# One decoder layer on one Trainium2 core: the order of work around three RMS norms, the opening products behind them, and the split of four weight blocks

## The chip, the cores and the metric

The kernel runs on one core of a Trainium2 chip (trn2). The metric is device time in microseconds (us) of one execution. A core has a matrix engine (PE in the profile), a vector engine (DVE), an activation engine (ACT), a general engine (POOL) and a sync engine (SP), each of which runs its own row of instructions in order, and 16 DMA engines. The profile shows a granted clock of the matrix engine (PEclk); 1.00 is its full 2.4 GHz, and the other level is 1.2 GHz.

## The reference

One layer on 512 prompt tokens and 8 x 4 sample tokens, 544 in all, with 1024 features: a half-step SwiGLU block, a mixer (RWKV-7 heads beside differential attention), a second SwiGLU block, and an RMS norm ahead of and behind each of the three.

```python
def rms_norm(x, g, eps):
    return x * lax.rsqrt(jnp.mean(x * x, axis=-1, keepdims=True) + eps) * g

def swiglu(x, w_in, w_out):
    gate, up = jnp.split(x @ w_in, 2, axis=-1)
    return (jax.nn.silu(gate) * up) @ w_out

def layer(x, l, shift0, wkv0, attend, P):
    g = P['norm_gains'][l]
    h = x + 0.5 * rms_norm(swiglu(rms_norm(x, g[0]), ff1_in, ff1_out), g[1])
    m, k, v, wkv, shift = mixer(rms_norm(h, g[2]), l, shift0, wkv0, attend, P)
    h = h + rms_norm(m, g[3])
    h = h + 0.5 * rms_norm(swiglu(rms_norm(h, g[4]), ff2_in, ff2_out), g[5])
    return h, k, v, wkv, shift
```

Here `D_FF` is 2816 and everything is fp32.

## The kernel before, in words

Features lie on partitions, tokens on the free axis. The 544 tokens are two halves of 272 (`HALF`), s = 0 and s = 1, and an activation is KB = 8 tiles of 128 x 272 for each half. Every fp32 product is made of three products of a rounded high part and a low part: high weight by high input, high weight by low input, low weight by high input.

**Weights.** `weights()` (L110 to L126) loads 128 x 1024 fp32 (512 KB) by SP into `wraw` (3 buffers), ACT copies it into the high part `whi` (L118), and DVE subtracts to get the low part `wlo` (L124). `whi` and `wlo` have 4 buffers each, so at most four blocks are ready at a time. With `added=True` the low part is made without DVE: ACT writes the negated copy (L121), and POOL issues a DMA that adds the weights from memory onto it (L122).

**Products.** `dot` (L134) is one 128-feature output for one half: 16 matmuls with `whi` (L138 with the high input `xh`, L139 with the low input `xl`), then 8 with `wlo` (L142), all into one PSUM bank. `acc_tile` hands out three PSUM banks in turn (names mm and pb). `mm3` (L128) is the same for a single tile.

**Norms.** For y, the output of a block, `Squares` accumulates squares (ACT squares, DVE or POOL adds, L236); the accumulators are `sqa0` and `sqa1`. `rstds` (L238) takes the sums over partitions with ones on PE (L176, 3 columns of tokens), computes 1/sqrt with ten small DVE instructions (`inv_sqrt`, L200 to L210, on 128 x 3) and spreads the result over partitions by PE transposes (`spread`, L222). `close_half` (L270) then does, tile by tile, norm (`pn`, L284), residual add into `h` (L285; POOL for tiles 0, 2, 4, 6, DVE for the others), the parts `xh` (ACT, L254) and `xl` (DVE, L256) of the next block's input, and the squares of the new h. These steps are a generator that later products advance (`tick`). The scale of the next norm is not put into the parts but applied to the products behind them. `Pre.scale` (L259) makes it: for the norms ahead of both SwiGLU blocks (`gi` 0 and 4) by one matmul with a 128 x 128 matrix of ones (L263) and `inv_sqrt` on the wide 128 x 272 form; for the mixer's norm (`gi` 2) by `rstds` and an ACT copy.

**What follows a norm.** `opening` (L316) is the first four products of the next block: for half 0 four whole dots, with half 1's norm steps advanced between them, then half 1 tile by tile in four banks (`mm3`). `after(...)` pins matmuls behind others on PE: `chain` holds the last transpose and the last sum matmul of half 1's norm. In `ff` the opening makes gate and up of output blocks j = 0 and 1; they are copied to SBUF, and scaled once the scale is there (L520, L521). Blocks j = 2 to 5 of the first group go one at a time: two weight blocks (gate, up), half 0, then half 1, and here DVE takes the products out of PSUM by a multiplication with the scale (L530, L531), which therefore has to be there. DVE then multiplies gate and up (L407), and the low part of the hidden tile is made (L151). `scaled` and `mixtures` (L372, L363, L365, L385) prepare tiles for the later groups.

**Order.** The Tile framework simulates the program and writes each engine's row from it, by priority and readiness, so the order on an engine is not the order of the text. The norm before ff2 lies behind `w_out` (L1378 to L1392: eight dots for half 0, eight for half 1; in half 1 the weights m > 3 have `added=True`).

Of the kernel before, what the change touches and what calls it, by code (L numbers as in the profile page):

```python
# [13 lines left out]
OP = mybir.AluOpType  # L14
# [38 lines left out]
def build(ctx, tc, A):  # L53
# [191 lines left out]
    class Pre:  # L245
# [12 lines left out]

        def scale(self, s):  # L259
            self.rs[s] = wk.tile([128, HALF], FT, name=f"rpre{s}", bufs=1)  # L260
            if self.gi != 2:
                ps = bank()
                T.matmul(ps[:, :HALF], ones, self.sq[s].acc, start=True, stop=True)  # L263
                inv_sqrt(ps, HALF, 1.0 / DM, NORM_EPS, y=self.rs[s])
            else:
                S.activation(self.rs[s], rstds(self.sq[s])[0], AF.Copy)
# [3 lines left out]
    def close_half(h, s, y, sq, gcol, pre=None, xp=None, spill=None, out=None, pool=True):  # L270

        drain()
        if s == 1 and pre is not None:
            with tc.high_priority():
                r, = rstds(sq)
            chain[:] = last
            pre.scale(0)
        else:
            r, = rstds(sq)

        def steps():
            for m in range(KB):
                t = wk.tile([128, HALF], FT, name="pn")
                V.scalar_tensor_tensor(t, y[s][m], gcol[:, m:m + 1], r, op0=OP.mult, op1=OP.mult)  # L284
                (G if m in ((0, 2, 4, 6) if out is None else (0, 2, 4)) else V).tensor_tensor(h[s][:, m], h[s][:, m], t, op=OP.add)  # L285
                if out is not None and (m % 2 or m == KB - 2):
                    q = m if m >= KB - 2 else m - 1
                    nc.sync.dma_start(out[s, :, q:m + 1], h[s][:, q:m + 1])
                if pre is not None:
                    pre.split(xp, h, s, m)  # L290
                    pre.sq[s].add(h[s][:, m], G if pool and s == 0 and m in (2, 4, 6) else V)
                if spill is not None and m % 2:
                    nc.scalar.dma_start(spill[s, :, m - 1:m + 1], h[s][:, m - 1:m + 1])
                yield
            if s == 1 and pre is not None:
                pre.scale(1)

        later.append(steps())

# [16 lines left out]
    def opening(ws, xs, take):  # L316

        for i, w in enumerate(ws):
            ps = acc_tile()
            with after(chain[1] if i == 1 else chain[0] if i == 2 else None):  # L320
                dot(ps, w, xs[0])
            take(0, i, ps)
            tick(3)
# [69 lines left out]
    def ff(win, wout, pre, h, done, xp, end, lead=(), begin=None):  # L393
        with ExitStack() as st:
# [112 lines left out]
            for gi, (j0, j1) in enumerate(GROUPS):  # L507
                if gi == 0:
# [9 lines left out]
                    for s in range(2):  # L518
                        for g, u in raw[s]:
                            V.tensor_tensor(g, g, pre.rs[s], op=OP.mult)  # L520
                            V.tensor_tensor(u, u, pre.rs[s], op=OP.mult)  # L521
                            hidden(s, g, u)
                    for j in range(2, j1):
                        ws = [weights(win[j, i], 1024) for i in range(2)]
                        for s in range(2):
                            pg, pu = acc_tile(), acc_tile()
                            for p, w in zip((pg, pu), ws):
                                dot(p, w, pre.xs[s])
                            g, u = gate_up()
                            V.tensor_tensor(g, pg, pre.rs[s], op=OP.mult)  # L530
                            V.tensor_tensor(u, pu, pre.rs[s], op=OP.mult)  # L531
                            hidden(s, g, u)
                            for _ in range(3 * (j > 2)):
                                next(scaled, None)
                else:
                    for j in range(j0, j1):
                        now = ahead or seven(j)
# [840 lines left out]
    def output(s):  # L1378
# [1 line left out]
            t = (s4 if j == 2 else c4)([128, 3, HALF], f"my{s}_{j}")  # L1380
            y[s].extend(t[:, m] for m in range(3))
        for m in range(KB):
            w = weights(A["w_out"][m], 1024, added=s == 1 and m > 3)
            ps = acc_tile()
            dot(ps, w, parts[s])
            S.activation(y[s][m], ps, AF.Copy)
# [172 lines left out]
```

## Time and profile before

| | us |
|---|---|
| median of three timed runs | 1233.25 (1227.38 to 1235.25) |
| the profiled execution | 1238.08 |
| its span in the trace | 1236.3 |
| PE busy | 1182.9 (96%) |
| DVE busy | 827.9 (67%) |
| ACT busy | 580.2 (47%) |
| POOL busy | 183.6 (15%) |

In the rows below times are us from the start of the span unless marked ns. A timeline row gives start, duration, engine, line, operation, output<-inputs, shapes and count; in brackets the idle time of the engine ahead of it and what ended it. A window row gives for a stretch the busy time of PE, the PE weight loads, DVE, ACT and POOL (with the number of instructions), then the granted clock, the DMA share and GB/s. Durations of neighbouring instructions of one engine overlap, since they are pipelined.

### The profile page before, as it was taken

The numbers are of one execution on the slowest core, as the hardware profiler recorded it, in microseconds if no ns is written. First come the engines' busy times: TensorE is split into PE (matmuls) and PEld (weight loads), VectorE is DVE, ScalarE is ACT, GpSimd is POOL, SyncE is SP. The second block draws the span as 40 slices with busy tenths as digits, with TensorE's granted clock in tenths as the row PEclk, the third lists the DMA queues.
The fourth block names the chain that finished last, engine by engine and source line by source line (L and its number), as shares of the span: only waits on it lengthen the run. The fifth ranks groups of instructions, "written<-read, shape, count | busy, mean of one in ns | idle before, by whom it ended". The sixth has DMA issues, their size and how long they took to land.

```text
span 1236.3 us, 25322 instructions
## 1 busy us (share of the span) xinstructions
PE 1182.9 (96%) x9970; PEld 1117.1 (90%) x9970; DVE 827.9 (67%) x1859; ACT 580.2 (47%) x1072; POOL 183.6 (15%) x249
## 2 busy tenths in 40 slices
PE   8999999999999999999998999979899999999995
PEld 8999999999998889989896645979899999999995
DVE  7983775856867568678325568858962775856766
ACT  7545543634543465633114536565344643634531
POOL 0002110201003255521000021121001110201002
PEclk8999999999998898999799999999899999999998
DMA  6338884866651567789316487571337984867531
GB/s 213 99 95 233 205 208 118 209 176 150 149 209 40 164 149 212 218 228 236 80 53 202 138 291 246 176 223 55 108 120 195 215 211 120 204 168 167 132 124 73
DMA packets 85628, 204.35 MB, mean 165 GB/s; under 512 B 9057, under 2 KB 20065, under 8 KB 84102
## 3 DMA queue, kind: packets, MB, share of 16 engines
q1 hardware_dynamic: 66150, 151.10, 36.9%
q0 software_dynamic: 17056, 47.19, 21.8%
q10 hardware_dynamic: 2304, 4.46, 1.0%
q8 instruction: 78, 1.28, 0.4%
q14 instruction: 40, 0.33, 0.1%
HBM read 185.08 MB, written 18.95 MB: 165 GB/s over the span
## 4 chain that ended last, share of the span: by engine, by line
PE 86%; DMA 5%; DVE 5%; issue 2%; ACT 1%; POOL 1%; SPq 0%; DVEq 0%; ACTq 0%; POOLq 0%
PE mm L138 10%; PE mm L139 10%; PE mm L142 9%; PE pb L460 7%; PE pb L461 6%; PE pb L463 6%; PE pb L142 4%; PE pb L138 4%; PE pb L139 4%; PE mm L463 3%; PE mm L461 3%; PE mm L460 3%; PE pb L923 1%; DMA t<-in_ff_in_dram 1%; DMA wlo<-in_w_out_dram 1%
## 5 line engine op out<-in xcount | busy, mean ns | idle before, releaser
L118 ACT ACTIVATE whi<-wraw 128x1024 fp32r<-128x1024 f32 (+2 forms) x128 | 118.0, 925 | 184.6 <-PE mm L139 104.9
L138 PE MATMUL mm<-xh,whi 128*128 128x272 f32 x472 | 131.9, 307 | 10.6 <-DVE ga L530 6.5
L139 PE MATMUL mm<-xl,whi 128*128 128x272 f32 x472 | 129.6, 303 | 2.6 <-DVE xl L256 2.6
L124 DVE TENSOR_TENSOR wlo<-wraw,whi 128x1024 fp32r<-128x1024 f32 (+2 forms) x102 | 102.9, 1011 | 34.0 <-ACT whi L118 30.6
L138 PEld LDWEIGHTS mm<-xh,whi 128*128 128x128 f32 x472 | 94.9, 201 | 13.1 <-ACT ga L406 6.8
L139 PEld LDWEIGHTS mm<-xl,whi 128*128 128x128 f32 x472 | 94.8, 201 | 4.3 <-DVE xl L256 3.9
L428 POOL DMA_DIRECT2D t<-in_ff_in_dram x32 | 38.6, 1206 | 385.0 <-DMA t<-in_ff_in_dram 211.0
L142 PE MATMUL mm<-xh,wlo 128*128 128x272 f32 x472 | 73.7, 297 | 2.3 <-DMA wlo<-in_w_in_dram 2.3
L474 DVE TENSOR_TENSOR ga<-pb,ga 128x272 f32<-128x272 f32 x139 | 60.5, 436 | 20.9 <-PE pb L463 18.5
L142 PEld LDWEIGHTS mm<-xh,wlo 128*128 128x128 f32 x472 | 66.2, 196 | 2.8 <-DMA wlo<-in_w_in_dram 2.6
L460 PE MATMUL pb<-sh,t1h 128*128 128x272 f32 x256 | 66.7, 289 | 2.1 <-ACT t1h L440 2.1
L461 PE MATMUL pb<-sl,t1h 128*128 128x272 f32 x256 | 66.6, 287 | 0.0
L440 ACT ACTIVATE t1h<-t 128x1024 fp32r<-128x1024 f32 x32 | 34.0, 1062 | 61.7 <-issue 33.2
L138 PE MATMUL pb<-xh,whi 128*128 128x272 f32 x232 | 61.8, 297 | 0.8 <-DVE vf L989 0.6
L562 DVE TENSOR_TENSOR y<-mm,y 128x272 f32<-128x272 f32 x64 | 28.1, 439 | 50.5 <-PE mm L142 50.0
L139 PE MATMUL pb<-xl,whi 128*128 128x272 f32 x232 | 61.5, 295 | 0.0
L139 PE MATMUL mm<-hd1l,whi 128*128 128x272 f32 x236 | 61.2, 288 | 0.0
L138 PE MATMUL mm<-hd1h,whi 128*128 128x272 f32 x236 | 61.0, 288 | 0.0
L139 PE MATMUL mm<-hd0l,whi 128*128 128x272 f32 x231 | 59.8, 288 | 0.0
L138 PE MATMUL mm<-hd0h,whi 128*128 128x272 f32 x231 | 59.4, 288 | 0.0
L450 POOL DMA_DIRECT2D wlo<-in_ff_in_dram x32 | 31.8, 993 | 182.6 <-ACT wlo L449 180.3
L460 PE MATMUL pb<-fa,whi 128*128 128x272 f32 x212 | 55.2, 288 | 0.0
(473 smaller groups left out, 3651.6 us busy)
## 6 DMA issues: line engine op xcount, KB each, us to landing
wraw<-in_ff_in_dram SPq DMA_DIRECT2D x55, 512.0 KB, 4.6
t<-in_ff_in_dram SPq DMA_DIRECT2D x64, 256.0 KB, 3.5
t<-in_ff_in_dram POOLq DMA_DIRECT2D x32, 512.0 KB, 5.8
wlo<-in_ff_in_dram POOLq DMA_DIRECT2D x32, 512.0 KB, 6.8
wraw<-in_w_in_dram SPq DMA_DIRECT2D x26, 512.0 KB, 7.3
wraw<-in_ff_out_dram SPq DMA_DIRECT2D x32, 384.0 KB, 3.0
wlo<-in_w_in_dram POOLq DMA_DIRECT2D x22, 512.0 KB, 8.7
wraw<-in_ff_out_dram SPq DMA_DIRECT2D x32, 320.0 KB, 3.2
```

What stands on the lines that cost most here:

```text
L118: S.activation(hi, raw, AF.Copy)
L124: V.tensor_tensor(lo, raw, hi.bitcast(FT), op=OP.subtract)
L138: T.matmul(ps, hi, xs[k][0], start=k == 0, stop=False)
L139: T.matmul(ps, hi, xs[k][1], start=False, stop=False)
L142: latest[0] = T.matmul(ps, wcols(w, k0 + k)[1], xs[k][0], start=False, stop=k == n - 1).ins
L428: G.dma_start(t1, bass.AP(tensor=src.tensor, offset=src.offset, ap=[[1024, 128], [128 * 1024 + 512, 2], [1, 512]]), accum_op=OP.add)
L440: S.activation(hi, src, AF.Copy)
L450: G.dma_start(lo, win[j, 0], accum_op=OP.add)
L460: T.matmul(ps, c, x[k][0], start=k == 0, stop=False)
L461: T.matmul(ps, c, x[k][1], start=False, stop=False)
L463: T.matmul(ps, wcols(w, n + k)[1], x[k][0], start=False, stop=k == KH - 1)
L474: V.tensor_tensor(dst, p, q, op=op)
```

## The change

1. `close_half`: norm, residual and parts of all eight tiles first, then the squares of h for all eight (16 steps instead of 8).
2. `Pre.scale`: the wide form is left for `gi` 0 only, so ff2's input norm takes `rstds` and an ACT copy.
3. `opening`: the first dot is pinned behind the sums of half 1's norm and the second behind its transposes (before: the second behind the sums, the third behind the transposes).
4. `ff`, first group: blocks j in twos. Four weight blocks are taken, half 0 of both blocks, then half 1 of both; `scaled` is advanced 4 times a step instead of 3.
5. `w_out`, half 1, m > 3: the low parts of the weights by DVE, as for the other blocks.

```diff
@@ Pre.scale
-            if self.gi != 2:
+            if self.gi == 0:
                 ps = bank()
                 T.matmul(ps[:, :HALF], ones, self.sq[s].acc, start=True, stop=True)
                 inv_sqrt(ps, HALF, 1.0 / DM, NORM_EPS, y=self.rs[s])
@@ close_half
                 if pre is not None:
                     pre.split(xp, h, s, m)
-                    pre.sq[s].add(h[s][:, m], G if pool and s == 0 and m in (2, 4, 6) else V)
                 if spill is not None and m % 2:
                     nc.scalar.dma_start(spill[s, :, m - 1:m + 1], h[s][:, m - 1:m + 1])
                 yield
-            if s == 1 and pre is not None:
-                pre.scale(1)
+            if pre is not None:
+                for m in range(KB):
+                    pre.sq[s].add(h[s][:, m], G if pool and s == 0 and m in (2, 4, 6) else V)
+                    yield
+                if s == 1:
+                    pre.scale(1)
@@ opening
-            with after(chain[1] if i == 1 else chain[0] if i == 2 else None):
+            with after(chain[1 - i] if i < 2 else None):
                 dot(ps, w, xs[0])
@@ ff
-                    for j in range(2, j1):
-                        ws = [weights(win[j, i], 1024) for i in range(2)]
+                    for j in range(2, j1, 2):
+                        ws = [[weights(win[i, n], 1024) for n in range(2)] for i in (j, j + 1)]
                         for s in range(2):
-                            pg, pu = acc_tile(), acc_tile()
-                            for p, w in zip((pg, pu), ws):
-                                dot(p, w, pre.xs[s])
...
-                            for _ in range(3 * (j > 2)):
-                                next(scaled, None)
+                            for both in ws:
+                                pg, pu = acc_tile(), acc_tile()
+                                for p, w in zip((pg, pu), both):
+                                    dot(p, w, pre.xs[s])
...
+                                for _ in range(4 * (j > 2)):
+                                    next(scaled, None)
@@ end of build
-            w = weights(A["w_out"][m], 1024, added=s == 1 and m > 3)
+            w = weights(A["w_out"][m], 1024)
```

Three places in the engines' rows show what moves; SP's row is the same in both kernels. Line numbers of the changed kernel are up to four higher from L300 on (L407 is L410 there, L530 is L534).

PE at the end of `w_out`, half 1, before (pb_10701 holds the sums of half 1's norm, mm_10661 the last product of `w_out`, mm_10814 and pb_10870 the first two of ff2's opening):

```order
L142 MATMUL mm_10814<-xh0_7_10693,wlo_10786 128x272
L142 MATMUL mm_10661<-orp1_9842,wlo_10658 128x272 x4
L142 MATMUL mm_10661<-oh1_9987,wlo_10658 128x272 x2
L142 MATMUL mm_10661<-oh1_10004,wlo_10658 128x272 x2
L176 MATMUL pb_10701<-ones_86,sqa1_10367 128x1 x3
L138 MATMUL pb_10870<-xh0_0_10372,whi_10790 128x272
```

And in the changed kernel (pb_10697 holds the sums, mm_10637 the last product of `w_out`, mm_10818 the first of the opening):

```order
L142 MATMUL mm_10637<-orp1_9842,wlo_10635 128x272 x4
L142 MATMUL mm_10637<-oh1_9987,wlo_10635 128x272 x2
L142 MATMUL mm_10637<-oh1_10004,wlo_10635 128x272 x2
L176 MATMUL pb_10697<-ones_86,sqa1_10367 128x1 x3
L138 MATMUL mm_10818<-xh0_0_10372,whi_10788 128x272
L139 MATMUL mm_10818<-xl0_0_10374,whi_10788 128x272
```

Before, a whole opening product stood ahead of the sums; now the sums follow the last `w_out` product at once.

PE at the transposes of the same norm, before (pb_10717 is their output, mm_10928 the third opening product):

```order
L142 MATMUL pb_10870<-xh0_6_10647,wlo_10792 128x272
L142 MATMUL pb_10870<-xh0_7_10693,wlo_10792 128x272
L222 MATMUL pb_10717<-cst_108,ry_10706 128x128 x3
L263 MATMUL pb_10722<-sqa0_10376,ones_86 128x272
```

And in the changed kernel (pb_10713 is their output, mm_10915 the second opening product, pb_10866 another one; `sqa0_10674` are the squares of h, half 0):

```order
L138 MATMUL mm_10915<-xh0_4_10542,whi_10800 128x272
L139 MATMUL mm_10915<-xl0_4_10544,whi_10800 128x272
L222 MATMUL pb_10713<-cst_108,ry_10702 128x128 x3
L176 MATMUL pb_10718<-ones_86,sqa0_10674 128x1 x3
L138 MATMUL pb_10866<-xh0_0_10372,whi_10794 128x272
```

Before, 24 matmuls stood between sums and transposes, and 48 of the opening's 96 matmuls for half 0 were done ahead of the transposes; now it is 34 and 34. The wide matmul L263 has become a 3-column sum (L176).

PE in ff2's first group, at the third product behind the opening, before (mm_11164 is the second product, of half 0; mm_11223 the third):

```order
L139 MATMUL mm_11164<-xl0_6_10649,whi_11159 128x272
L138 MATMUL mm_11164<-xh0_7_10693,whi_11159 128x272
L139 MATMUL mm_11164<-xl0_7_10695,whi_11159 128x272
L138 MATMUL mm_11223<-xh1_0_10843,whi_11153 128x272
L139 MATMUL mm_11223<-xl1_0_10845,whi_11153 128x272
L138 MATMUL mm_11223<-xh1_1_10852,whi_11153 128x272
```

And in the changed kernel (mm_11188 is the second, mm_11247 the third):

```order
L139 MATMUL mm_11188<-xl0_6_10629,whi_11171 128x272
L138 MATMUL mm_11188<-xh0_7_10669,whi_11171 128x272
L139 MATMUL mm_11188<-xl0_7_10671,whi_11171 128x272
L138 MATMUL mm_11247<-xh0_0_10372,whi_11177 128x272
L139 MATMUL mm_11247<-xl0_0_10374,whi_11177 128x272
L138 MATMUL mm_11247<-xh0_1_10414,whi_11177 128x272
```

Before, the third product is of half 1 with the first weight block again; now it is of half 0 with the third weight block, and half 1 comes after four products.

DVE at the scale of half 1 in ff2 (`rpre`, 128 x 272), before:

```order
L124 TENSOR_TENSOR wlo<-wraw,whi 128x1024
L151 TENSOR_TENSOR hd0l<-up,hd0h 128x272
L200 TENSOR_SCALAR wv<-pb 128x272
L203 TENSOR_SCALAR rpre_10975<-wv 128x272
L204 TENSOR_TENSOR wt<-wv,rpre_10975 128x272
L205 TENSOR_TENSOR wt<-wt,rpre_10975 128x272
L206 SCALAR_TENSOR_TENSOR wt<-wt 128x272
L207 SCALAR_TENSOR_TENSOR rpre_10975<-wt,rpre_10975 128x272
```

And in the changed kernel (`rv`, `rt` and `ry` are the small tiles of `inv_sqrt`):

```order
L204 TENSOR_TENSOR rt<-rv,ry 128x3
L124 TENSOR_TENSOR wlo<-wraw,whi 128x1024 x2
L205 TENSOR_TENSOR rt<-rt,ry 128x3
L206 SCALAR_TENSOR_TENSOR rt<-rt 128x3
L207 SCALAR_TENSOR_TENSOR ry<-rt,ry 128x3
L534 TENSOR_TENSOR ga<-pb,rpre_10717 128x272
L208 TENSOR_TENSOR rt<-rv,ry 128x3
L124 TENSOR_TENSOR wlo<-wraw,whi 128x1024
L209 SCALAR_TENSOR_TENSOR rt<-rt,ry 128x3
L535 TENSOR_TENSOR up<-mm,rpre_10717 128x272
L210 SCALAR_TENSOR_TENSOR ry<-rt,ry 128x3
```

Before, nine wide instructions follow one another ahead of every multiplication with this scale; now they are small ones, mixed with evacuations that need the scale of half 0 (`rpre_10717`) and with weight parts (L124).

## Rows read from the trace of the kernel before

**Rows 1.** The page: busy time of PE, and the chain that ended last by engine.

```profile
PE 1182.9 (96%) x9970; PEld 1117.1 (90%) x9970; DVE 827.9 (67%) x1859; ACT 580.2 (47%) x1072; POOL 183.6 (15%) x249
...
PE 86%; DMA 5%; DVE 5%; issue 2%; ACT 1%; POOL 1%; SPq 0%; DVEq 0%; ACTq 0%; POOLq 0%
```

**Rows 2.** Windows of 10 us (columns as in the section on the profile).

```profile
390.00:400.00 10.00, 7.56 (x30) 6.73 (x31) 7.87 (x22) 4.15 (x11) 3.37 (x4) 0.60 0.15 56
...
820.00:830.00 10.00, 6.05 (x34) 5.83 (x35) 4.96 (x8) 4.88 (x11) 0.00 (x0) 0.83 0.96 281
...
850.00:860.00 10.00, 10.00 (x82) 10.00 (x81) 10.00 (x25) 7.32 (x17) 0.91 (x1) 1.00 0.15 56
880.00:890.00 10.00, 7.09 (x43) 7.12 (x44) 9.93 (x27) 4.50 (x12) 0.00 (x0) 0.66 0.01 2
```

**Rows 3.** What PE waited for from 795 to 945 us: total, times, longest.

```profile
PE mm L138 <- DVE ga L530: 5.7, 1, 5.7
PE pb L142 <- DMA wlo<-in_w_out_dram: 3.2, 1, 3.2
PE pb L176 <- DVE sqa L236: 3.0, 1, 3.0
PE mm L142 <- DMA wlo<-in_w_out_dram: 2.9, 2, 1.8
PE pb L460 <- ACT t1h L440: 2.1, 1, 2.1
```

**Rows 4.** Timeline of PE, five places.

```profile
53.92 0.36 PE L138 MATMUL mm<-xh,whi 128*128 128x272 f32 x1 [0.79 <-DVE ga L530]
...
825.22 0.46 PE L142 MATMUL pb<-orp,wlo 128*128 128x272 f32 x1 [3.24 <-DMA wlo<-in_w_out_dram]
...
837.07 0.58 PE L176 MATMUL pb<-ones,sqa 128*128 128x1 f32 x4 [3.05 <-DVE sqa L236]
...
842.23 0.50 PE L222 MATMUL pb<-cst,ry 128*128 128x128 f32 x2
...
882.91 0.56 PE L138 MATMUL mm<-xh,whi 128*128 128x272 f32 x1 [5.68 <-DVE ga L530]
```

**Rows 5.** Timeline of DVE, eight places.

```profile
403.43 0.50 DVE L284 SCALAR_TENSOR_TENSOR pn<-y,hgains,pb 128x272 f32<-128x272 f32 x1 [3.61 <-PE pb L222]
...
807.69 0.85 DVE L285 TENSOR_TENSOR h<-h,pn 128x272 f32<-128x272 f32 x1
...
813.88 0.43 DVE L285 TENSOR_TENSOR h<-h,pn 128x272 f32<-128x272 f32 x1
...
839.48 0.16 DVE L210 SCALAR_TENSOR_TENSOR ry<-rt,ry 128x3 f32<-128x3 f32 x1
...
842.88 0.50 DVE L284 SCALAR_TENSOR_TENSOR pn<-my,gains,pb 128x272 f32<-128x272 f32 x1 [3.24 <-PE pb L222]
...
869.58 1.22 DVE L124 TENSOR_TENSOR wlo<-wraw,whi 128x1024 fp32r<-128x1024 f32 x1
...
876.77 0.44 DVE L200 TENSOR_SCALAR wv<-pb 128x272 f32<-128x272 f32 x1 [1.04 <-PE pb L263]
...
880.44 0.44 DVE L210 SCALAR_TENSOR_TENSOR rpre<-wt,rpre 128x272 f32<-128x272 f32 x1
```

**Rows 6.** DVE instructions by line and shape, 780 to 920 us: busy, mean ns.

```profile
L124 DVE TENSOR_TENSOR wlo<-wraw,whi 128x1024 fp32r<-128x1024 f32 x18 | 22.1, 1228 | 8.1 <-ACT whi L118 6.2 <-PE mm L142 1.7
L236 DVE TENSOR_TENSOR sqa<-sqa,sq 128x272 f32<-128x272 f32 x28 | 12.3, 448 | 3.7 <-ACT sq L235 3.4
L256 DVE SCALAR_TENSOR_TENSOR xl<-h,gains,xh 128x272 fp32r<-128x272 f32 x16 | 7.5, 491 | 0.3 <-ACT xh L254 0.3
L284 DVE SCALAR_TENSOR_TENSOR pn<-my,gains,pb 128x272 f32<-128x272 f32 x16 | 7.3, 490 | 6.6 <-PE pb L222 6.6
...
L285 DVE TENSOR_TENSOR h<-h,pn 128x272 f32<-128x272 f32 x8 | 4.5, 565 | 0.1
```

**Rows 7.** POOL instructions by line and shape, the same stretch.

```profile
L285 POOL TENSOR_TENSOR h<-h,pn 128x272 f32<-128x272 f32 x8 | 6.7, 833 | 32.1 <-DVE pn L284 32.0
```

More of the change, by code (lines that the diff above doesn't have):

```diff
@@ L522, in ff @@
                             hidden(s, g, u)
-                    for j in range(2, j1):
-                        ws = [weights(win[j, i], 1024) for i in range(2)]
+                    for j in range(2, j1, 2):
+                        ws = [[weights(win[i, n], 1024) for n in range(2)] for i in (j, j + 1)]
                         for s in range(2):
-                            pg, pu = acc_tile(), acc_tile()
-                            for p, w in zip((pg, pu), ws):
-                                dot(p, w, pre.xs[s])
[L529 to L532, printed above, removed]
-                            for _ in range(3 * (j > 2)):
-                                next(scaled, None)
+                            for both in ws:
+                                pg, pu = acc_tile(), acc_tile()
+                                for p, w in zip((pg, pu), both):
+                                    dot(p, w, pre.xs[s])
+                                g, u = gate_up()
+                                V.tensor_tensor(g, pg, pre.rs[s], op=OP.mult)
+                                V.tensor_tensor(u, pu, pre.rs[s], op=OP.mult)
+                                hidden(s, g, u)
+                                for _ in range(4 * (j > 2)):
+                                    next(scaled, None)
                 else:
```

## The prediction

> **What bounds the kernel now.** I read the page first: PE is busy for 1182.9 us, 96% of the span, and the chain of waits runs through PE for 86%, through DMA and DVE for 5% each [rows 1]. So a change can only help where PE stands still or runs slowly, and about 50 us of the 1236.3 are idle. The second view is the table of windows, to find these places. Full speed is seen from 850 to 860 us: 82 matmuls in 10.00 us, 0.122 us each, clock 1.00 [rows 2]. Three stretches stand out: 390 to 400 (PE busy 7.56, clock 0.60), 820 to 830 (6.05, 0.83) and 880 to 890 (7.09, 0.66) [rows 2]. They are the norm between ff1 and the mixer, the norm between the mixer and ff2, and the scale of ff2's half 1. In each, PE stood idle, and then the granted clock fell toward the 1.2 GHz level: from 390 to 400 one matmul took 7.56 / 30 = 0.252 us, twice 0.122. An idle stretch of some us therefore costs more than itself. The third view, the waits of PE from 795 to 945, names who ended them: 5.7 us for DVE at L530, 3.2 and 2.9 for the low weight parts of `w_out` by DMA, 3.0 for the squares, and 2.1 at L460 [rows 3]. The timeline gives the places: 825.22 for a low part, 837.07 for the sums, 882.91 for the scale [rows 4]. The change touches all of these but the last in the list of waits (L460).
>
> **The change, part by part.** Sums are made against the profiled execution (1238.08 us, span 1236.3); the median is 1233.25, so I subtract the same gain from it (the ratio of the two, 0.996, alters a gain of 18 us by less than 0.1).
>
> *ff1.* PE waits 0.79 us at 53.92 for L530 of a half-1 product, that is for half 1's scale [rows 4]. With blocks in twos the first half-1 evacuation comes two products (48 matmuls, 5.9 us) later. The wait goes: 0.8 us. The scale stays wide here (`gi` 0).
>
> *Norm between ff1 and the mixer.* The squares of h no longer stand ahead of the last squares of y in DVE's row: in the order, y's last square for half 1 stands four places earlier, 4 x 0.448 us [rows 6] = 1.8 us. From 390 to 400 PE idles 10 - 7.56 = 2.4 us and loses 30 x (0.252 - 0.122) = 3.9 us to the clock [rows 2]. DVE gets the spread norm at 403.43 after waiting 3.61 us for PE's transposes [rows 5]. In the changed order 33 matmuls stand between sums and transposes instead of 24, at 0.252 us another 2.3 us, but that is work that PE has to do anyway. The gain lies between 0 (the longer way eats it) and 4; I take 1.3, since only the 1.8 are certain to be released.
>
> *The end of `w_out`.* Four low parts go from ACT, POOL and DMA to DVE. PE's waits of 3.2 + 2.9 = 6.1 us [rows 3] go, if DVE is in time. Before, the last `w_out` matmul ends where PE begins to wait for the sums, at 837.07 - 3.05 = 834.0 [rows 4]. Without 6.1 us of waits, without the ff2 product that stood ahead of the sums (24 x 0.122 = 2.9), and without the clock loss of 820 to 830 (6.05 - 34 x 0.122 = 1.9 [rows 2]), it ends at 823.1. DVE has to be through with y's half 1 squares for the sums. From its first norm instructions (807.69 less the two ahead of it, 806.8 [rows 5]) the changed order has, up to the last of these squares, 6 low parts, 8 norms, 4 residuals, 7 `xl` and 7 squares: 6 x 1.228 + 8 x 0.490 + 4 x 0.565 + 7 x 0.491 + 7 x 0.448 = 20.1 us [rows 6], so 826.9 by these means, somewhat less since neighbours overlap. I take 826. PE waits for it about 3 us, as before (3.05), but 11 us earlier. Between sums and transposes stand 34 matmuls: 4.1 us at full clock, 8.6 at half. The small root needs from the start of the sums to the end of L210 839.48 + 0.16 - 837.07 = 2.6 us [rows 4, 5] and is hidden by them. With 0.7 us for the sums the transposes are out between 830.9 and 835.3; I take the middle, 833, since before, this stretch ran partly at half clock. Before, they were out at 842.88, when DVE's wait ends [rows 5] (L222 itself starts at 842.23 [rows 4]). That is 9.9 us earlier, but 62 instead of 48 of half 0's 96 opening matmuls are still to do: 14 x 0.122 = 1.7 us back. Gain 8.2 us, between 5.9 and 10.3.
>
> A price in this term is open: the four low parts now run on DVE while POOL adds residuals. At 807.69 a DVE residual took 0.85 us, the same instruction at 813.88 took 0.43 [rows 5]; if each of the four low parts is delayed once like that, the cost is 4 x 0.42 = 1.7 us, and it falls into the 3 us for which PE waits anyway, so it moves the sums. The Trainium skill (page "SBUF — State Buffer", section "Who interferes with whom") states a harder rule that speaks against this change: a DVE instruction with two SBUF inputs and a GpSimd instruction exclude each other for the whole instruction. By it each new low part could wait for a whole POOL residual, 0.833 us [rows 7], 3.3 us in all; the gain of this term would be 4.9 instead of 8.2, and the time 3.3 us higher than by the sum below. The pair of rows at 807.69 and 813.88 shows only half of that per meeting, and I do not take it off.
>
> *The scale of ff2.* Half 1: after the ones matmul, DVE goes through nine wide instructions, 876.77 to 880.44 + 0.44, 4.1 us, then four multiplications and the evacuations, and PE waits 5.68 us until 882.91 for a bank [rows 4, 5]; after it the clock is at 0.66 and 43 matmuls take 7.09 us, 1.85 over 43 x 0.122 [rows 2]. In the changed kernel the first evacuation that needs this scale comes four products behind the opening instead of two, and the nine instructions are small ones (0.16 us each at 839.48 [rows 5]). The gain is 5.7 + 1.8 = 7.5, if DVE is through in time. Check: before, DVE is fully busy from 842.88 to the fourth low part's end at 869.58 + 1.22 = 870.8, 27.9 us [rows 5]; the window from 850 to 860 shows 10.00 busy [rows 2]. The same instructions in the changed kernel lose nine wide ones (about 3.4 us less, small ones being 0.16) and gain a second small root (1.8), three squares (1.3) and an evacuation (0.4): 28.0 us. PE reaches the transposes of scale 1 some 250 matmuls behind those of the norm, 30.5 us. So DVE has 2 to 3 us to spare, and this is the thinnest point of the forecast. The bounds of this term are 7.5 and, if DVE is some 5 us late instead, 2.5.
>
> *Sum.* 0.8 + 1.3 + 8.2 + 7.5 = 17.8 us. The profiled execution would fall to 1220.3, the median to 1233.25 - 17.8 = 1215.5. Unchanged, I take it, are 2.1 us at L460 [rows 3] and everything else; fewer DMAs (four adding ones less) run beside the loads.
>
> **The rivals.**
>
> *A: half the gain, DVE becomes the bound.* For it: DVE is fully busy from 850 to 860 and 9.93 of 10 from 880 to 890 [rows 2], takes four more low parts, and the low parts waited 8.1 us for ACT in 18 [rows 6], 0.45 each. If the sums come 3.3 us late (POOL), the way to the transposes runs wholly at half clock (2.3 more than the middle) and scale 1 comes 4.5 us late, 10 of the 17.8 us are lost: 1225.5. Against it: the wide instructions leave DVE twice, for half 0 and half 1.
>
> *B: no change.* The saved time comes back as waits for loads: all later weights are wanted 18 us earlier, and DMA already ends 5% of the chain [rows 1], with a DMA share of 0.96 from 820 to 830 [rows 2]. Time 1233. Against it: the share is 0.15 from 850 to 860, 0.01 from 880 to 890 [rows 2], so the loads have room behind the norm.
>
> *C: slower.* Blocks in twos hold all four weight buffers. The first buffer is free only after the fifth of eight products, and its block for j = 4 is wanted 72 matmuls, 8.8 us, later. ACT's copy and DVE's 1.23 [rows 6] have to pass in that time, behind what stands in DVE's row. If DVE is over some 6.6 us behind there, PE waits at each of the eight blocks of ff1 and ff2 from j = 4 on for a round trip: 2.2 us for ACT and DVE and 0.9 of lowered clock, 8 x 3.1 = 25 us against 17.8 gained: 1240. For it: DVE full at 880 to 890. Against it: three products' time (8.8 us) is four times the 2.2 us of the way, and from 850 to 860, with DVE as full, PE did not stop [rows 2].
>
> **How the numbers follow.** The forecast has 0.62, A 0.23, B 0.08, C 0.07. The forecast's own range is 1208 to 1222 (terms 5.9 to 10.3, 0 to 4 and down to 5); A reaches to 1229. The range 1206 to 1229 leaves out B, C and a small rest. About 1% (12.3 us) is what a measurement of this kernel can tell from no change. Faster by more: 0.57 of the forecast's 0.62 and 0.07 of A, 0.64. Within 1%: 0.05, 0.16 of A, 0.07 of B and 0.01 of C, 0.29. Slower: 0.07, most of C and a little of B.
>
> **What would show it.** Right: no wait for `wlo<-in_w_out_dram`; the sums near 826, the transposes near 833; no wait at L530's successor, L534, over 1 us in ff2; the window behind it at clock 1.00. Wrong: DVE still in y's squares at 829; PE waiting for DVE at the transposes or at L534 near 865 to 875; waits for `whi` or `wlo` at j = 4; or the same PE waits in the w_in and the ff2 loads, longer than before.

## The result, and the profile after

The changed kernel takes 1218.12 us (median of four runs, 1214.82 to 1221.15) where the kernel before takes 1230.55 (four runs): a ratio of 0.9895, 95% interval 0.9849 to 0.9942. Two later series gave 0.9895 (0.985 to 0.9939; 1216.85 against 1228.97) and 0.9881 (0.9848 to 0.9914; 1214.68 against 1227.84). So the gain is 12 to 13 us. The forecast was 1215.5, a gain of 17.8, range 1206 to 1229. It was counted from a median of 1233.25 of three runs; with the fourth run that median is 1230.55, and in the later series 1228 to 1229. So the time is met more closely than the gain, and in part by this luck.

The profiled execution of the changed kernel has a span of 1217.0 us, the first one of before 1236.3. These two traces differ by 19 us, more than the medians do, and the second trace of before and the mixer's clock, both below, say why. The page of the changed kernel, busy times and chain:

```profile
PE 1173.3 (96%) x9984; PEld 1108.6 (91%) x9984; DVE 825.7 (68%) x1863; ACT 577.0 (47%) x1070; POOL 180.4 (15%) x245
...
PE 86%; DVE 7%; DMA 4%; ACT 2%; issue 1%; POOL 0%; SPq 0%; DVEq 0%; ACTq 0%
```

PE's busy share is unchanged, and DVE has a larger part of the chain than before (7% against 5%, [rows 1]): what PE waits for is now mostly DVE.

The windows that answer to [rows 2]; the stretch from 830 to 840 is ff2's opening, 860 to 870 is where the scale of half 1 comes in:

```profile
390.00:400.00 10.00, 8.99 (x74) 9.02 (x74) 7.75 (x24) 4.59 (x11) 3.40 (x5) 1.00 0.12 45
820.00:830.00 10.00, 9.39 (x56) 9.42 (x57) 6.15 (x23) 2.90 (x7) 0.70 (x1) 0.69 0.32 114
830.00:840.00 10.00, 10.00 (x82) 10.00 (x81) 10.00 (x31) 7.31 (x19) 3.15 (x4) 1.00 0.26 93
860.00:870.00 10.00, 10.00 (x83) 10.00 (x82) 7.91 (x20) 5.91 (x13) 0.00 (x0) 1.00 0.17 51
```

From 390 to 400 and 860 to 870 PE is at full clock, where before the same stages had 0.60 and 0.66. At the first norm the low clock comes later instead, from 410 to 420; the first line is of before, the second of the changed kernel:

```profile
410.00:420.00 10.00, 7.55 (x33) 6.70 (x32) 8.12 (x32) 5.76 (x15) 5.06 (x13) 0.62 0.77 230
```

```profile
410.00:420.00 10.00, 9.33 (x41) 8.80 (x40) 5.37 (x22) 4.86 (x13) 0.00 (x0) 0.50 0.69 206
```

At the end of `w_out` PE is not at full clock: 820 to 830 has 56 matmuls in 9.39 us, 0.168 us each, clock 0.69. The first opening matmul behind the sums starts at 821.88, and two windows part what follows, up to the transposes at 828.14:

```profile
821.90:826.10 4.20, 4.20 (x19) 4.20 (x20) 3.02 (x14) 1.44 (x4) 0.00 (x0) 0.50 0.33 124
826.10:828.10 2.00, 2.00 (x17) 2.00 (x17) 0.00 (x0) 0.40 (x1) 0.00 (x0) 0.99 0.00 0
```

So 18 of the 34 matmuls ran at half clock and 16 at full clock (a window also counts the matmuls that it cuts). What PE waited for from 780 to 930 us, to be set beside [rows 3]:

```profile
PE pb L176 <- DVE sqa L236: 4.0, 1, 4.0
PE pb L463 <- ACT t1h L443: 1.8, 1, 1.8
PE pb L138 <- ACT ga L518: 0.2, 1, 0.2
```

The low parts of `w_out` and the evacuation at ff2's scale are gone from the list. The wait for the squares has grown from 3.0 to 4.0 us. Six places of PE's timeline, answering to [rows 4]; L176 takes the sums of a norm, L222 transposes:

```profile
391.01 0.36 PE L138 MATMUL pb<-xh,whi 128*128 128x272 f32 x1 [3.05 <-DVE y L566]
...
392.96 0.72 PE L176 MATMUL pb<-ones,sqa 128*128 128x1 f32 x6
...
397.76 0.49 PE L222 MATMUL pb<-cst,ry 128*128 128x128 f32 x3
...
820.61 1.20 PE L176 MATMUL pb<-ones,sqa 128*128 128x1 f32 x5 [3.97 <-DVE sqa L236]
...
828.14 0.49 PE L222 MATMUL pb<-cst,ry 128*128 128x128 f32 x3
...
861.74 0.49 PE L222 MATMUL pb<-cst,ry 128*128 128x128 f32 x3
```

The sums of the norm behind `w_out` start at 820.61, its transposes at 828.14; the transposes of the scale of half 1 at 861.74 wait for nothing. At 391.01 there is a wait that the kernel before did not have. Its sums and transposes of the first norm came later:

```profile
396.78 1.27 PE L176 MATMUL pb<-ones,sqa 128*128 128x1 f32 x6
...
402.90 0.49 PE L222 MATMUL pb<-cst,ry 128*128 128x128 f32 x3
```

DVE in the changed kernel at six places, answering to [rows 5]:

```profile
802.29 1.60 DVE L124 TENSOR_TENSOR wlo<-wraw,whi 128x1024 fp32r<-128x1024 f32 x1
...
805.34 1.01 DVE L236 TENSOR_TENSOR sqa<-sqa,sq 128x272 f32<-128x272 f32 x1
...
808.99 1.01 DVE L285 TENSOR_TENSOR h<-h,pn 128x272 f32<-128x272 f32 x1
...
812.64 1.42 DVE L256 SCALAR_TENSOR_TENSOR xl<-h,gains,xh 128x272 fp32r<-128x272 f32 x2
...
828.67 0.50 DVE L284 SCALAR_TENSOR_TENSOR pn<-my,gains,pb 128x272 f32<-128x272 f32 x1 [3.50 <-PE pb L222]
...
859.18 0.15 DVE L210 SCALAR_TENSOR_TENSOR ry<-rt,ry 128x3 f32<-128x3 f32 x1
```

DVE receives the transposes at 828.67 and has the second small root done at 859.18 + 0.15 = 859.33, 2.4 us before PE reads it at 861.74. (This root is nine instructions, L200 to L210, and not ten.) The first four rows are read with POOL's residuals at the same time:

```profile
802.04 0.77 POOL L285 TENSOR_TENSOR h<-h,pn 128x272 f32<-128x272 f32 x1 [18.47 <-DVE pn L284]
805.09 0.96 POOL L285 TENSOR_TENSOR h<-h,pn 128x272 f32<-128x272 f32 x1 [2.27 <-DVE pn L284]
808.80 0.90 POOL L285 TENSOR_TENSOR h<-h,pn 128x272 f32<-128x272 f32 x1 [2.75 <-DVE pn L284]
812.79 0.97 POOL L285 TENSOR_TENSOR h<-h,pn 128x272 f32<-128x272 f32 x1 [3.09 <-DVE pn L284]
```

POOL's add at 805.09 ends at 806.05, and the DVE square that began at 805.34 ends at 806.35, 0.30 later; at 809.70 and 810.00 the next pair ends alike. The kernel before has such rows too, beside the one at 807.69 [rows 5]:

```profile
809.51 0.72 DVE L285 TENSOR_TENSOR h<-h,pn 128x272 f32<-128x272 f32 x1
...
811.08 0.77 DVE L285 TENSOR_TENSOR h<-h,pn 128x272 f32<-128x272 f32 x1
...
812.71 0.83 DVE L236 TENSOR_TENSOR sqa<-sqa,sq 128x272 f32<-128x272 f32 x1
```

### The profile page after: what moved, and what is told of

It reads as the page before. It is cut to its first block, busy times and chain, and to the rows that moved or that the text cites. A ratio compares the mean times of both kernels' runs of the same rounds, so it can differ in the third digit from the quotient of the medians.

```text
span 1217.0 us, 25368 instructions
## 1 busy us (share of the span) xinstructions
PE 1173.3 (96%) x9984; PEld 1108.6 (91%) x9984; DVE 825.7 (68%) x1863; ACT 577.0 (47%) x1070; POOL 180.4 (15%) x245
## 4 chain that ended last, share of the span: by engine, by line
PE 86%; DVE 7%; DMA 4%; ACT 2%; issue 1%; POOL 0%; SPq 0%; DVEq 0%; ACTq 0%
PE mm L138 9%; PE mm L139 9%; PE mm L142 9%; PE pb L463 7%; PE pb L464 7%; PE pb L466 7%; PE pb L138 5%; PE pb L139 5%; PE pb L142 4%; PE mm L466 3%; PE mm L464 3%; PE mm L463 3%; PE pb L927 1%; DVE pn L284 1%; PE mm L1265 1%
## 5 line engine op out<-in xcount | busy, mean ns | idle before, releaser
L138 PE MATMUL mm<-xh,whi 128*128 128x272 f32 x472 | 128.5, 302 | 3.6 <-ACT whi L587 2.0
L124 DVE TENSOR_TENSOR wlo<-wraw,whi 128x1024 fp32r<-128x1024 f32 (+2 forms) x106 | 108.0, 1022 | 28.9 <-ACT whi L118 25.4
L139 PE MATMUL mm<-xl,whi 128*128 128x272 f32 x472 | 125.9, 297 | 0.0
L138 PEld LDWEIGHTS mm<-xh,whi 128*128 128x128 f32 x472 | 92.4, 196 | 5.6 <-ACT whi L587 2.2
L431 POOL DMA_DIRECT2D t<-in_ff_in_dram x32 | 38.6, 1206 | 380.1 <-DMA t<-in_ff_in_dram 195.4
L139 PEld LDWEIGHTS mm<-xl,whi 128*128 128x128 f32 x472 | 92.3, 196 | 0.6 <-DVE xl L256 0.3
```

Source lines behind the costliest of these rows:

```text
L124: V.tensor_tensor(lo, raw, hi.bitcast(FT), op=OP.subtract)
L138: T.matmul(ps, hi, xs[k][0], start=k == 0, stop=False)
L139: T.matmul(ps, hi, xs[k][1], start=False, stop=False)
L431: G.dma_start(t1, bass.AP(tensor=src.tensor, offset=src.offset, ap=[[1024, 128], [128 * 1024 + 512, 2], [1, 512]]), accum_op=OP.add)
```

## The experiments

All kernels were timed against the kernel before on the same chip. For the traces a second measure is used: the start of the same matmul in two timelines, and how much the difference changes over a stage. Three stages are needed: A, the first norm and the input projections (374 to 490 us in the first trace of before); B, a stretch of the mixer that no edit touches (590 to 612); C, from the end of `w_out` to the end of ff2's first group (800 to 925). Negative is faster than the first trace of before.

| kernel | median, us | ratio to before (95%) | A | B | C | clock, 595 to 605 |
|---|---|---|---|---|---|---|
| before, first trace | 1230.55 | 1 | 0 | 0 | 0 | 0.59 |
| e5 before, second trace | 1229.39 | 1.0017 (0.9993 to 1.0041) | -3.6 | -8.4 | +1.1 | 1.00 |
| changed, first trace | 1218.12 | 0.9895 (0.9849 to 0.9942) | -4.6 | -0.4 | -13.1 | 0.54 |
| e1 changed, second | 1216.85 | 0.9895 (0.985 to 0.9939) | -3.1 | -1.0 | -13.1 | 0.51 |
| e9 changed, third | 1214.68 | 0.9881 (0.9848 to 0.9914) | -3.4 | -0.2 | -12.6 | 0.50 |
| e2 split back | 1224.58 | 0.9962 (0.9934 to 0.9989) | -2.5 | -1.9 | -6.8 | 0.56 |
| e3 wide scale back | 1217.90 | 0.9895 (0.9857 to 0.9933) | -3.0 | -0.8 | -13.5 | 0.50 |
| e4 blocks one by one | 1221.04 | 0.9919 (0.9887 to 0.9952) | -3.6 | -1.0 | -12.6 | 0.50 |
| e7 both of e3 and e4 | 1222.69 | 0.9957 (0.9933 to 0.9981) | -1.4 | -1.9 | -7.6 | 0.54 |
| e8 squares back | 1215.18 | 0.9880 (0.9841 to 0.9918) | -3.2 | -8.0 | -9.9 | 1.00 |
| e6 pins back | 1212.15 | 0.9867 (0.9832 to 0.9901) | -4.8 | -0.2 | -17.5 | 0.60 |
| e11 pins back, again | 1215.39 | 0.9885 (0.9848 to 0.9922) | -4.7 | -0.8 | -14.5 | 0.54 |
| e10 before, split alone | 1223.34 | 0.9963 (0.9938 to 0.9988) | -4.8 | -7.3 | -7.1 | 1.00 |
| e12 pins back, first squares back | 1213.03 | 0.9870 (0.9835 to 0.9906) | -0.8 | -7.9 | -17.6 | 1.00 |

**The changed kernel twice more.** No edit.

> The changed kernel once more, with more rounds. If the stage gains read from the two traces (0.8 us in ff1, 1.6 at the first norm, 6.4 at the end of w_out, 6.7 at ff2's scale, 15.5 in sum) are all there is, the median lies 14 to 17 us below the kernel before. If the pair of traces flatters the change, because the profiled execution of before (1238.08) lay 7.5 us above its median, the median is only 10 to 13 us lower and the stage gains of other executions are smaller too.

> The changed kernel beside the next three on one chip. Theory (its time is the same on every chip relative to before): ratio 0.988 to 0.991. In its trace the mixer's stretch near 590 to 605 us is what moves most between executions: at clock 0.5 in part of it (as in the two traces of this kernel so far) the span is 1217 or more, at 1.00 it is 1208 to 1212. Rival (the change itself slows that stretch): it is at 0.5 again.

Measured: 12.1 and 13.2 us under before. The first lies in the second range of its expectation (10 to 13), though not for its reason: stage C is the same within 0.5 us in all three traces, so that part of the gain is firm. The second is inside its theory (0.9881). In the third trace the mixer's stretch ran at 0.50 again and the span was 1218.2: that is what both expected of such a trace, so it decides nothing between them; what does is taken up below.

**The split alone, undone and done.** In e2 the changed kernel gets the old line back, in e10 the kernel before gets the new one:

```diff
-            w = weights(A["w_out"][m], 1024)
+            w = weights(A["w_out"][m], 1024, added=s == 1 and m > 3)
```

> The changed kernel with the low parts of w_out's last four weight blocks again by ACT and an adding DMA. Theory (the DMA waits are what the end of w_out gained): PE waits about 6 us for wlo<-in_w_out_dram again, and the kernel is 4 to 8 us slower than the changed one. Rival (DVE, full from 800 to 820 in the changed kernel, is the bound there, and with four low parts less it has the squares ready earlier): the waits come back, but PE's 4.0 us for the squares go, so at most 2 us slower.

> The kernel before with the fifth edit alone: the low parts of w_out's last four weight blocks by DVE. Theory (this edit carries half of the gain or more, as undoing it cost 8 of 13 us): the DMA waits of 5 to 6 us go, PE's wait for the squares does not grow over 5 us, the 5.7 us wait at ff2's scale stays, 5 to 9 us faster than before. Rival (without the squares moved, DVE's four more low parts make the squares later by what the DMA waits were): within 2 us of before.

Undone, the ratio goes to 0.9962, about 8 us slower than the changed kernel, and stage C loses 6.3 us. The waits of PE from 780 to 930 us in e2:

```profile
PE pb L142 <- DMA wlo<-in_w_out_dram: 3.2, 1, 3.2
PE pb L176 <- DVE sqa L236: 3.1, 1, 3.1
PE mm L142 <- DMA wlo<-in_w_out_dram: 2.3, 1, 2.3
```

The two DMA waits are back with 5.5 us, and the wait for the squares is 0.9 shorter than in the changed kernel (4.0), not gone: the theory holds, and the rival's trade is a sixth of it. Done alone on the kernel before, stage C gains 7.1 us against the first trace of before and 8.2 against the second, but the median only 4.5 (ratio 0.9963), just under what the theory expected. From e10, the same view:

```profile
PE mm L138 <- DVE ga L530: 5.7, 1, 5.7
PE mm L139 <- DVE xl L256: 2.5, 2, 1.5
...
PE pb L176 <- DVE sqa L236: 0.3, 1, 0.3
```

With the old pins a whole opening product stands ahead of the sums, and the wait for the squares is 0.3 us. But PE waits 2.5 us for input parts (`xl`), which before it did not: DVE's four low parts do make it later, as the rival had it, and this gives back a part of the 6.1 us. The wait at ff2's scale is untouched, as it should be. By time this edit alone is some third of the gain, not half.

**The two edits at ff2's scale, each undone, and both.** e3 is the first of these pieces, e4 the second, e7 both:

```diff
-            if self.gi == 0:
+            if self.gi != 2:
...
-                    for j in range(2, j1, 2):
-                        ws = [[weights(win[i, n], 1024) for n in range(2)] for i in (j, j + 1)]
+                    for j in range(2, j1):
+                        ws = [weights(win[j, i], 1024) for i in range(2)]
```

(the second with the loop body of before.)

> The changed kernel with the wide root for both halves of ff2's input norm. Theory (scale 1 has 2.4 us to spare on DVE before PE's transposes; the wide form adds some 3.4 us for half 0 and 2.4 for half 1): PE waits 1 to 4 us at the first evacuations of half 1 near 865 us, 1 to 5 us slower. Rival (blocks in twos alone remove the wait, by moving the need for scale 1 two products later): under 1 us.

> The changed kernel with blocks j one at a time again. Theory (both edits together remove the 5.7 us wait and its slow clock; the small root alone is not early enough, since in the changed kernel scale 1 is ready near 863 us and would be wanted near 856): PE waits 4 to 7 us in ff2, and 0.8 us more in ff1, 5 to 9 us slower. Rival (the small root alone removes it): 1 us slower or less.

> The changed kernel with both the wide root in ff2 and the blocks one by one. Theory (either edit alone removes the wait at ff2's scale, as the two runs with one of them undone had it: so only with both undone it comes back): PE waits 4 to 6 us for DVE at L533 in ff2 again, and the kernel is 5 to 8 us slower than with the blocks alone undone (1221.0), about 1226 to 1229. Rival (what each costs simply adds, 1.0 and 4.2): 1222.

With the wide root back nothing is lost: ratio 0.9895, stage C -13.5. With blocks one by one stage C loses 0.5 us at most, and PE does not wait for the scale there; so in both runs the rival was right about ff2, and my theories fell. What e4 loses (ratio 0.9919, some 3 us, with intervals that overlap) lies elsewhere in its trace. Some 1.5 us are in ff1, where the scale is wide in every kernel and the wait is back:

```profile
PE mm L138 <- DVE ga L533: 1.3, 1, 1.3
```

Another 2 us come just behind stage C: PE waits 2.5 us for a tile that ACT makes (`t1h`), where the changed kernel waits 1.8, and runs at a lower clock behind it (0.83, where the changed kernel has 1.00):

```profile
920.00:930.00 10.00, 10.00 (x70) 10.00 (x69) 1.73 (x2) 2.88 (x6) 0.00 (x0) 0.83 0.67 169
```

And in e7, from 780 to 930 us:

```profile
PE pb L176 <- DVE sqa L236: 3.9, 1, 3.9
PE mm L138 <- DVE ga L533: 3.1, 1, 3.1
```

The wait is back with both edits undone, shorter than the 5.7 of before, and the clock behind it is low (columns as before: 61 matmuls in 10 us):

```profile
870.00:880.00 10.00, 10.00 (x61) 10.00 (x61) 9.09 (x24) 4.20 (x10) 0.00 (x0) 0.71 0.01 2
```

Stage C loses 5.3 us against the changed kernel, and the ratio of e7 is 0.0038 above that of e4, 4.7 us. Both the wait (3.1) and the price (4.7) stay under the theory's 4 to 6 and 5 to 8. The medians alone (1222.69 and 1221.04, of two series) would have said 1.7 and the rival, and the intervals of the two ratios overlap. It is the traces, one of each kernel, that say that each edit alone removes this wait, and that it is back with both undone. That it is 3.1 and not the 5.7 of before must come from the other three edits; no run parts them.

**The pins back**, alone and with the first norm's squares back (e12):

```diff
-            with after(chain[1 - i] if i < 2 else None):
+            with after(chain[1] if i == 1 else chain[0] if i == 2 else None):
```

> The changed kernel with the opening's pins as before: 15 matmuls of the first opening product stand ahead of the sums at the end of w_out, 34 between sums and transposes. Theory (DVE sets when the squares are ready, PE waits 3.9 us for them, and the low clock behind that wait stretches the 34 matmuls): PE fills 1.8 of the 3.9 us, the transposes come no later, and the kernel is 1 to 4 us faster than the changed one. Rival (the pins do what the changed kernel gains at the two norms): 2 us slower or more.

> The changed kernel with the opening's pins as before, beside the changed kernel on one chip. Theory (15 matmuls ahead of the sums fill PE's wait, and the clock stays at full speed up to the transposes): 3 to 5 us faster than the changed kernel. Rival (the first run was a lucky one): within 2 us of it.

> The changed kernel with the pins as before and the squares of h back inside the loop at the first norm (the mixer's input) alone. Theory (with the squares back everywhere the first norm was 2 us shorter and the second 3 us longer than in the changed kernel): 1 to 3 us faster than with the pins back alone. Rival (the 2 us at the first norm were the clock's): within 1 us of it.

In e6 PE works on the first opening product while DVE finishes the squares. Its waits from 780 to 930 us:

```profile
PE mm L139 <- DVE xl L256: 0.7, 1, 0.7
PE pb L176 <- DVE sqa L236: 0.6, 1, 0.6
```

The 4.0 us became 0.6 (and 0.7 for an input part), and the window behind the sums:

```profile
820.00:830.00 10.00, 10.00 (x83) 10.00 (x82) 8.74 (x30) 5.99 (x16) 2.46 (x3) 1.00 0.31 108
```

That is full clock with 83 matmuls, against 56 in the changed kernel, and stage C gains 4.4 us more. The same kernel in e11, the same view:

```profile
820.00:830.00 10.00, 10.00 (x61) 10.00 (x62) 5.61 (x22) 3.45 (x9) 0.87 (x2) 0.70 0.20 68
```

The waits were the same, but the clock fell here, and stage C gained 1.4 to 1.9 us. By time, e6 was 1.3% faster than before and e11 1.15%, with the changed kernel at 1.05 to 1.2%: the intervals overlap. On the chip they shared, e11 was 0.7 us slower than the changed kernel by median (1215.39 against 1214.68), so there the rival holds. All three traces with the old pins (e6, e11, e12) show the shorter wait; whether the time follows depends on the clock, and that is not settled. e12 has the lowest median on its chip, 1213.03, 2.4 us under e11 and 1.65 under the changed kernel, also within the intervals. What e12 did not do is shorten the first norm: its stage A is -0.8. Its gain over e11 is in stage B (7.1 us) and C (3.1), less 3.9 in A: the size that the theory gave, and not for its reason.

**The squares back inside the loop** (e8): the squares return to the loop over tiles at both norms.

```diff
                     pre.split(xp, h, s, m)
+                    pre.sq[s].add(h[s][:, m], G if pool and s == 0 and m in (2, 4, 6) else V)
```

> The changed kernel with the squares of h back inside the loop over tiles. Theory (DVE is full ahead of the sums at the end of w_out, and the squares of h stand among the squares of y): the sums there come 1 to 3 us later, 1 to 4 us slower. Rival (the scheduler's order puts the squares of y first in any case): under 1 us.

From e8's waits, 780 to 930 us:

```profile
PE pb L176 <- DVE sqa L236: 6.3, 1, 6.3
```

The wait for the squares grew from 4.0 to 6.3 us, and stage C lost 3.2: the theory of the order is right at this norm. But the median is 1215.18, no worse than the changed kernel (0.9880 against 0.9881 to 0.9895). Its trace was 7 us faster in stage B; that this holds for its median too is not shown.

**The kernel before once more.** No edit.

> The kernel before once more, for a second trace of it. Theory (its first profiled execution was a long one, 1238.08 against a median of 1229 over all timed runs, by lowered clock in the mixer, where 470 to 480 us ran at 0.69): the span is 1226 to 1234, the three waits of the norms (5.7, 6.1 and 3.0 us) are there again with the same lengths within 0.5, and the difference to the first trace lies in stretches that the change does not touch. Rival (the long execution is the usual one): span 1235 to 1240.

The span was 1226.6, at the low end of the theory, and the waits were the same (5.7, 3.2 and 3.0 us) but for the DMA waits of 2.9 us, which were 1.7. The 9.7 us to the first trace lie in stages A (3.6) and B (8.4), less some 2 us that it loses in ff1 and in stage C. The expectation had the right sort of place (the mixer's clock) and only half of it: 470 to 480, in stage A, was the smaller one.

**The mixer's clock.** Stage B has two forms. A window of it in the changed kernel, in the second trace of before, and in e12:

```profile
595.00:605.00 10.00, 10.00 (x87) 9.04 (x87) 3.01 (x5) 0.60 (x1) 0.00 (x0) 0.54 0.01 2
```

```profile
595.00:605.00 10.00, 10.00 (x124) 8.96 (x124) 3.88 (x7) 1.65 (x4) 0.00 (x0) 1.00 0.22 69
```

```profile
595.00:605.00 10.00, 10.00 (x120) 8.90 (x119) 3.61 (x7) 1.57 (x3) 0.00 (x0) 1.00 0.22 69
```

87 matmuls in 10 us at clock 0.54, against 124 and 120 at 1.00. Ahead of it PE stood for some time at one line, and the profile names nothing that it waited for. In the changed kernel:

```profile
PE pb L892 <- issue: 2.1, 1, 2.1
```

And in e12:

```profile
PE pb L894 <- issue: 0.6, 1, 0.6
```

In all 14 traces the two go together: where this gap was 1.5 us or more (2.5 in the first trace of before, 1.5 to 2.3 in nine others) the clock fell to 0.50 to 0.60; where it was 1.1 or less (none in e5, 0.4 in e8, 1.1 in e10, 0.6 in e12) it stayed at 1.00. And nine of the ten low ones are all the kernels with the first norm's squares behind the loop; of the five with the squares inside the loop only the first trace of before is low. PE's row is the same there in all kernels. So the squares edit goes with a slow mixer, in 9 of 9 traces against 1 of 5. How an edit 200 us earlier does that is open: no run moved that gap alone.

The traces say more of the gap itself. In the changed kernel the matmul behind it, and the one packet of the queue named instruction that the DMA view shows from 587.4 to 587.8 us:

```profile
589.94 0.69 PE L892 MATMUL pb<-ld,tmp 32*32 32x32 f32 x30 [2.05 <-issue]
```

```profile
q8 instruction: 1, 0.02, 15.2%
```

The packet (16 KB) starts at 587.59, and PE goes on 2.35 us later. In all 14 traces the gap, where there is one, stands ahead of the same matmul, and that matmul starts 2.2 to 2.6 us behind the start of such a packet. The packet is what comes early or late: 3.0 to 4.2 us after the matmul 128 places ahead of this one in the four traces with gaps of 1.1 us or less, 4.6 to 5.7 us in the other ten. This fits a PE that waits for its own instructions. It is read from times only, and what delays the packet in one group of kernels is not known.

## Why the prediction was right, step by step

The time was in the range and on the right side; the gain was forecast at 17.8 us and measured at 12 to 13. By stages, taking the means of the three traces of the changed kernel and the two of before:

- **ff1** (forecast 0.8): the wait of 0.79 us is gone, and there the changed kernel gains 1.0 us on the first trace of before in each of its three traces; up to 374 us, where stage A begins, it is 1.0 us under the first trace of before and 2.4 under the second. That blocks in twos do it is shown by e4, where the wait is back with 1.3 us.
- **First norm** (forecast 1.3, 0 to 4): stage A is -3.7 on average against -1.8, so 1.9. The way there was another than argued. In the first pair of traces the sums came at 392.96 and not 396.78, the transposes at 397.76 and not 402.90, 4 to 5 us earlier, 0.7 of which the changed kernel brought along. Against that stands a new wait of 3.05 us at 391.01 for DVE's addition into y, since the first opening product that PE now takes needs the bank which that addition frees. The new pins bring it: e8 has it too (3.3), and e6, e11 and e12, with the old pins, do not, but wait 2.0 to 3.2 us for input parts (`xl`) there. A part of the lead is lost behind the transposes, where the clock is 0.50 from 410 to 420. That the squares gave this gain, as the prediction has it, is not borne out: e8, with the squares back, keeps it (stage A -3.2). The traces of one kernel differ here by as much as the gain, so which edit gives it stays open.
- **End of `w_out`** (forecast 8.2, 5.9 to 10.3): the changed kernel enters this stage 5.95 us ahead. On the clock of before, the last product ended at 816.64 + 5.95 = 822.6 (forecast 823.1), the sums came at 820.61 + 5.95 = 826.6 (826), and the transposes were with DVE at 828.67 + 5.95 = 834.6 (833). The term is 842.88 - 834.6 - 1.7 = 6.6. The middle between full and half clock was about right: the 34 matmuls took 828.14 - 821.88 = 6.3 us, where the middle of 4.1 and 8.6 is 6.35. The missing 1.6 us lie around them: the sums came 0.6 late, the stretch from the sums to the first opening matmul took 821.88 - 820.61 = 1.3 us and not 0.7, and the prediction set the start of the transposes (833) against the time at which DVE had them (842.88), which leaves out the 0.5 us from 828.14 to 828.67. The sums were hit with some luck. From its first norm instruction to the last square of half 1, DVE took from 801.47 to 820.46, 19.0 us, where the forecast had 20.1 by means and 19.2 after a deduction for overlap. By the plain durations the same 32 instructions sum to 19.3 us; the overlap of neighbours took off some 2.4, more than was deducted, and POOL put 2.1 back.
- **DVE beside POOL there** (the price left open, 1.7 or 3.3). The four POOL adds cost DVE 0.39, 0.58, 0.58 and 0.52 us over the plain durations, 2.1 us (the rows from 802.29 to 812.64, where a plain low part takes 1.21, two plain `xl` 0.90 and a square or a residual 0.43). But this is hardly the price of the change: one of the four is a low part, and the kernel before paid much the same with other instructions, three residuals (0.85, 0.72 and 0.77 us) and a square (0.83) over a plain 0.43, 1.5 us in all. So the change added 0.6 us. At 805.34 and 808.99 the DVE instruction began behind POOL's add, by 0.25 and 0.19 us, and ended 0.30 us after it, as if it had stood still until then. The Trainium skill (page "SBUF — State Buffer", section "Who interferes with whom") states the rule: a DVE instruction with two SBUF inputs and a GpSimd instruction that reads SBUF exclude each other, and the one that starts second stands still until the other is done. The trace agrees with it in these pairs. The price was lower than 3.3 because DVE lost only what was left of each add.
- **Scale of ff2** (forecast 7.5, down to 2.5): stage C is -12.9 against a mean of +0.6 for before, 13.5 in all; less 6.6 leaves 6.9. DVE had 2.4 us to spare at the transposes, where 2 to 3 were forecast. What the forecast had wrong is the share of the edits: it asked for the blocks in twos and the small root together, and beside the other three edits either is enough (e3, e4, e7).
- **What was left out.** The touched stages gain 17 us in the traces (some 1.7, 1.9 and 13.5), close to the 17.8 forecast. The rest is stage B: -0.5 on average for the changed kernel, -4.2 for before, 3.7 us lost, and 17.1 - 3.7 is 13.4, where the medians say 12 to 13. Two traces of before are few for such a mean; e10, whose program is that of before up to there, had -7.3. The step that failed is the one that said "everything else" is unchanged: it costed the untouched mixer at nothing, while its clock moves stage B by up to 8 us from execution to execution, and it was low in all three traces of the changed kernel. That the medians are short of the forecast for this reason fits the traces and is not shown for the other executions.

Of the rivals, A had the right bottleneck, DVE as the bound ahead of the sums, and its size (1225.5) was too large. B and C did not come: no wait of PE for a load or a weight part was over 1 us longer than before, and no product of the blocks j = 4 and 5 waited for a weight.

In the traces the pins are the edit that does not pay where it was priced: they make PE wait where an opening product could run. The version without them and with the first norm's squares inside the loop (e12) had the lowest span of all traces, 1207.9 us, but no interval separates it from the changed kernel.

## What to carry to other kernels

A wait of the bottleneck engine is best priced with the clock behind it, and then by bounds: behind each wait of 3.0 to 6.3 us at the sums of the norm ahead of ff2 and at ff2's scale (14 in 11 traces) 14 to 26 matmuls ran at half speed, which cost 1.5 to 2.7 us more; behind the wait of 3 us at the first norm it was anything from 0.4 to 3.7 us. When two edits aim at one wait, undo each alone and then both, since each may be enough and neither then shows a price. And compare more than one trace of each kernel, stage by stage, before a difference is put down to an edit: one untouched stretch moved by 8 us between two traces of one kernel, as much as the largest term.

## What was not expected of the hardware

A stretch of small matmuls in the mixer, whose order no edit changes, runs at a granted clock of 0.50 to 0.60 or of 1.00, some 7 us apart. In the 14 traces it was the low one behind each gap of 1.5 to 2.5 us that the profile ascribes to nothing but the engine's own issue, and behind none of 0 to 1.1 us; and PE went on 2.2 to 2.6 us after a 16 KB packet of the instruction queue had started.
